# Moving casts, sums and weight preparation in a hybrid encoder layer: seven edits to a hand-ordered kernel

## The chip, the cores and the metric

The kernel runs on one NeuronCore of a Trainium2 chip. The metric is the device time of one execution in microseconds (us). Engines are named as in the profile: PE multiplies matrices, ACT (ScalarE), DVE (VectorE) and POOL (GpSimd) work elementwise, SP issues nearly all DMAs. Each engine works through its own instructions in the program's order; they wait for each other through semaphores.

## The reference

One layer of a bidirectional hybrid encoder over 1024 tokens of width 1024, in fp32:

```python
h = rmsnorm(x, norm_mix); proj = h @ w_in
q, k, v, r, lr_f, lr_b, u, g_a, g_b = split(proj)
# branch A: gated linear attention, 4 heads, forward and backward scan over chunks, summed
o = (gla_chunked(q, k, v, decay_f) + flip(gla_chunked(flip(q), ...)))
o = headnorm(o) * gla_norm * silu(r);  y_a = o @ w_branch_gla
# branch B: centred mean over windows 2/4/8/16 minus the token, a small matmul per group of channels
y_b = einsum('blgc,gcd->blgd', multiscale_pool(u), w_pool_group) * pool_scale
x = x + (sigmoid(g_a) * y_a + sigmoid(g_b) * y_b) @ w_out
gate, up = split(rmsnorm(x, norm_ffn) @ w_ffn_in)
x = x + (silu(gate) * up) @ w_ffn_out          # hidden width 2816
out = rmsnorm(x, norm_final)
```

## The kernel before, in words

**Products.** Every fp32 operand is cut into a high part (a cast on ACT) and a low part (operand minus high part, on DVE or POOL); `products` (L268) issues three matmuls for a pair: high by high, high by low, low by high, and `mm3` adds a call of `pump`. Large products use a seven-product form of 2 by 2 block multiplication: products number 1 to 7, each on sums or differences of blocks. Each product is 12 or 24 matmuls of 128x512.

**Who sets the order.** The order of all engines is written out by hand (`manual_schedule`). The main program issues products; work beside them is issued by generators that `pump(dt)` advances as matmuls are issued: `side` (attention, pooling), `aside` (the job lists of `prepare_beside`, one step every so many units), `pending` (weight casts) and `put_off` (`soon(delay, step)`). `settle()` issues all that was put off, `finish_side()` and `finish_beside()` all that is left of the generators.

**Slots.** Big tiles come from one pool of 39 slots. A tile that is allocated takes the slot of an older one, and its first writer waits for the last reader of that older one.

**Stages and places of the change.**

- *Attention, one head after the other (35 to 385 us).* `advance` (L758) makes the state of the next chunk: `st` on DVE, then on ACT the copy for use (`sb` or `sf`, L772) and the one to carry on (`so`, L773). `transposed_keys` (L750) makes `kt`: transposes on PE into `kp`, cast on ACT, low part on DVE. After the backward states come the scores, whose cast is `p`.
- *Gate units 0 to 9 (388 to 580 us).* Each unit is 128 columns of `w_in`, loaded as two `fraw` tiles, as seven products (`Gates.run`). Products 1, 6, 5 end in the ACT copy `ga<-ps` (L1304), which empties the bank for a later product. Units 6 to 9 also apply the pooled features: `load_pooled(g)` loads the tiles `ph` and `pl` from DRAM (L1245) and `Gates.pooling` multiplies them (`yb`). `flush` sends finished rows to DRAM (`sa_out`, `yb_out`, L501).
- *READY units.* The first two units of the FFN are prepared during the gate units: `unit_jobs` (L535) loads two `fraw` tiles of `w_ffn_in`, makes sums in them on POOL (L636), and `beside` cuts them into `uph` (ACT, L630) and `upl` (DVE, L621) and stores them in DRAM (`u_out`, L617), from where the FFN stage later loads them.
- *Branch and merged products (580 to 755 us)*: `line_make` (L1122) cuts the next piece into parts; `merged_piece` (L1204) makes sums of the merged rows `mg` (L1217 to L1219); `dh` and `dl` are the parts.
- *FFN (755 to 1180 us).* `features` (L1521) transposes the normed rows `xn` into banks `tr`, copies them to `hb` on ACT (L1535), makes block sums on DVE (L1547, L1550) and cuts them into `gh` (`cast_block`, ACT, L1513) and `gl` (`low_block`).
- *FFN output (1185 to 1377 us).* Pieces of weights (`wor`) and features (`gor`) are loaded (`load_piece`) and cut (`split_piece`) into `oh` and `ol`; `collect` adds the sums to `x` (L1860); `whole` (L1819) norms and stores the first four row blocks (`n3rs`, L1587; `scaled`, L1815; store, L1835) in steps put off with `soon`; `first_half` and `second_half` do the others.

Of the kernel before, what the change touches and what calls it, by code (L numbers as in the profile page):

```python
# [51 lines left out]
def kernel(  # L52
# [614 lines left out]
    def attention(h, q, k):  # L667
# [89 lines left out]

        def advance(old, n, d, kt, dst):  # L758

            kv = bank(ps_g, "kv")  # L760
            products(kv[:, :DV], tokens((kt[:, 0, :], kt[:, 1, :]), n), value(n))
            new = s1((DV,), "st")[:, :]
            after = factor(n, d, "after")
            if old is None:
                nc.vector.tensor_scalar(new, kv[:, :DV], after, None, op0=ALU.mult)
            else:
                nc.vector.scalar_tensor_tensor(
                    new, kv[:, :DV], after, old[:, :], op0=ALU.mult, op1=ALU.add
                )
            following = n + 1 if d == 0 else n - 1  # L770
            old = s1((DV,), "so")
            nc.scalar.activation(dst, new, AF.Copy, scale=factor(following, d, "before"))  # L772
            nc.scalar.activation(old[:, :], new, AF.Copy, scale=factor(following, d, "whole"))  # L773
            return old
# [45 lines left out]
        for n in range(NT - 1, 0, -1):  # L820
            m = n - 1
            old = advance(old, n, 1, kts[n // 4, 1], sb[m // 4][:, m % 4, :])
            if n == 7:
                apply_decay(1, 0)
            yield 1.2
            if n == 2:
                kts[0, 0] = transposed_keys(0, 0)
                yield 0.5
# [5 lines left out]
        for n in range(NT):  # L834
# [8 lines left out]
            for j, (a, b) in enumerate(terms):  # L843
                if j == len(terms) - 1 and n < NT - 1:
                    sf = s1((DV,), "sf")
                    old = advance(old, n, 0, kts[half, 0], sf[:, :])
                nc.tensor.matmul(op[:, :DV], a, b, start=False, stop=j == len(terms) - 1)
# [274 lines left out]
    def line_make():  # L1122
        n = len(made)
        if n < len(line):
            while len(loads) <= n:
                line_load()
            while len(begun_sums) <= n:
                line_sums()
            made.append(line[n][2](loads[n]))
# [74 lines left out]
    def merged_piece(p, c):  # L1204
# [6 lines left out]
        def sums():  # L1211
# [3 lines left out]
            if p == 6:  # L1215
                s3s.append(slot(s="s3"))
                sub(s3s[c][:, :, :], block(0, 0), block(1, 0))  # L1217
                padd(block(1, 0), block(1, 0), block(1, 1))
                sub(block(0, 0), block(1, 0), block(0, 0))  # L1219
            elif p == 3:  # L1220
# [124 lines left out]
    for n, run in enumerate(gate_runs):  # L1345
        zs[n] = Gates(n)
        last = n == len(gate_units) - 1
        if n == 0:
            prepare_beside(map(output_jobs, range(4)), 2.8)
        if n == 7:  # L1350
            finish_side()
            finish_beside()
            prepare_beside(map(unit_jobs, range(READY)), 3.1, 1, 2)
        if last:
            finish_beside()
        for at, (of, p) in enumerate(run):
            if not gates_ahead.step() and at in (5, 7):
                line_make()
            if n >= 6 and at == 2 and not last:
                load_pooled(n - 6)  # L1360
# [160 lines left out]
    def features(half):  # L1521
# [4 lines left out]
        def block(i, j, c):  # L1526
            return blocks[i, j][c][:, :, :]

        for k in range(KT):
            ps = bank(ps_g, "tr")  # L1530
            for i in range(4):
# [4 lines left out]
                blocks[k // 4, half][k % 4 // 2][:, k % 2, :], ps[:, :], AF.Copy, scale=g_ffn[:, k : k + 1]  # L1536
            )
            i = k % 4 // 2
            if k % 2 and half == 0:
# [3 lines left out]
            elif k % 2:  # L1543

                t = block(0, 0, i)
                if k < 4:
                    sub(t, block(0, 1, i), t)  # L1547
                    cast_block(5, i, t)
                else:
                    sub(t, block(1, 1, i), t)  # L1550
                    cast_block(6, i, t)
            elif half and k in (2, 4):
# [266 lines left out]
    def whole(ts):  # L1819
# [16 lines left out]

        steps = [(at + 9 * n, step, t) for n, t in enumerate(ts) for at, step in ((1, scale), (6, finish), (14.5, store))]
        for at, step, t in sorted(steps, key=lambda e: e[0]):
# [42 lines left out]
    for at, p in enumerate(OUT_ORDER):  # L1881
# [4 lines left out]
        for i in range(CLOSE if closing else n_of):  # L1886
# [6 lines left out]
            for m in range(4):  # L1893
# [3 lines left out]
                if m == (3 if i == n_of - 1 else 1):  # L1897
                    split_piece()

                if m == 3 and len(pieces) - n_of + CLOSE > n + 1 >= len(pieces) - 2 * CLOSE:  # L1900
                    load_piece()
# [36 lines left out]
```

## Time and profile before

| what | us |
|---|---|
| median of 3 runs (1389.67 to 1391.16) | 1390.08 |
| the profiled execution's own time | 1389.48 |
| its span in the trace | 1387.7 |
| PE busy | 1365.6 (98%) |
| DVE, POOL, ACT busy | 842.6, 752.6, 644.9 |
| mean granted clock of PE, share of full | 0.999 |

All times of the trace count from the start of the span. Rows of groups give the line of the kernel, the engine, the operation, what it writes and reads by the program's names with the number of instructions, then the shortest, median and longest duration in ns and the first and last start in us within the window asked for. Rows of waits give who waits for whom, us in total, times, the longest.

### The profile page before, as it was taken

Reading aid. Unit: us, or ns where it says so; the run is one execution under the profiler, and the core shown is the slowest. Engines: PE = TensorE matmul, PEld = TensorE weight load, DVE = VectorE, ACT = ScalarE, POOL = GpSimd, SP = SyncE. Lnnn points to the kernel's source line nnn. Section 1 sums busy time; section 2 is a strip of 40 time slices with the busy share of each in tenths; the row PEclk is TensorE's granted clock in tenths of the full one; section 3 lists DMA queues with packets and bytes.
Section 4 is the critical chain, followed back from the end, with each engine's and each line's share of the span. In section 5 each row is a group of like instructions: output and inputs, shape, how many; then the busy total and the mean of one; then the engine's idle time right before and its main releaser. Section 6 shows DMA issues by size and latency. Waiting matters only on the chain. (4 is left out here: it accounts for less than half of the span.)

```text
span 1387.7 us, 18162 instructions
## 1 busy us (share of the span) xinstructions
PE 1365.6 (98%) x6485; PEld 1143.0 (82%) x6485; DVE 842.6 (61%) x1018; ACT 644.9 (46%) x1176; POOL 752.6 (54%) x556
## 2 busy tenths in 40 slices
PE   7999999999999999999999999999999999999998
PEld 6888998988888888788887788888888888888876
DVE  6364656557835875687873866555655556344384
ACT  6465766655334544554347533333333334443253
POOL 3222617132288546668655276666666667554354
PEclk9999999999999999999999999999999999999999
DMA  6112414312478677996516355555444447966452
GB/s 224 31 47 60 142 52 134 105 55 77 137 214 288 198 228 242 369 405 224 186 61 241 116 175 175 174 175 175 148 146 142 145 140 273 390 244 215 169 209 93
DMA packets 166586, 243.60 MB, mean 176 GB/s; under 512 B 10936, under 2 KB 95968, under 8 KB 166496
## 3 DMA queue, kind: packets, MB, share of 16 engines
q1 hardware_dynamic: 166352, 242.18, 51.7%
q8 instruction: 51, 0.84, 0.2%
q14 instruction: 39, 0.32, 0.1%
q10 hardware_dynamic: 144, 0.26, 0.0%
HBM read 164.55 MB, written 77.86 MB: 175 GB/s over the span
## 5 line engine op out<-in xcount | busy, mean ns | idle before, releaser
L198 POOL TENSOR_TENSOR wl<-fs,wh 128x512 fp32r<-128x512 f32 x120 | 167.0, 1395 | 152.5 <-ACT wh L197 100.2
L271 PE MATMUL ps<-gh,wh 128*128 128x512 f32 x616 | 240.4, 390 | 0.0
L271 PE MATMUL ps<-gl,wh 128*128 128x512 f32 x616 | 239.8, 389 | 0.0
L271 PE MATMUL ps<-gh,wl 128*128 128x512 f32 x616 | 239.7, 389 | 0.0
L198 POOL TENSOR_TENSOR wl<-fraw,wh 128x512 fp32r<-128x512 f32 x90 | 128.8, 1432 | 64.4 <-ACT wh L197 62.0
L271 PE MATMUL ps<-hh,wh 128*128 128x512 f32 x376 | 151.6, 403 | 0.0
L198 POOL TENSOR_TENSOR ol<-gor,oh 128x1024 fp32r<-128x1024 f32 (+1 forms) x42 | 103.1, 2461 | 84.2 <-ACT oh L197 67.5
L271 PE MATMUL ps<-hh,wl 128*128 128x512 f32 x376 | 146.9, 391 | 0.6 <-POOL wl L198 0.6
L271 PE MATMUL ps<-hl,wh 128*128 128x512 f32 x376 | 146.6, 390 | 0.0
L271 PEld LDWEIGHTS ps<-gl,wh 128*128 128x128 f32 x616 | 115.7, 188 | 24.0 <-DVE gl L1517 0.3
L271 PEld LDWEIGHTS ps<-gh,wl 128*128 128x128 f32 x616 | 115.6, 188 | 23.9
L271 PEld LDWEIGHTS ps<-gh,wh 128*128 128x128 f32 x616 | 115.7, 188 | 23.8
L271 PE MATMUL ps<-oh,oh 128*128 128x512 f32 x308 | 119.9, 389 | 0.9 <-DVE x L1860 0.9
L271 PE MATMUL ps<-oh,ol 128*128 128x512 f32 x308 | 119.8, 389 | 0.0
L271 PE MATMUL ps<-ol,oh 128*128 128x512 f32 x308 | 119.8, 389 | 0.0
L198 POOL TENSOR_TENSOR wl<-raw,wh 128x512 fp32r<-128x512 f32 x40 | 54.5, 1374 | 117.0 <-ACT wh L197 108.7
L198 POOL TENSOR_TENSOR wl<-wraw,wh 128x512 fp32r<-128x512 f32 x56 | 89.9, 1633 | 45.6 <-ACT wh L197 36.4
L198 DVE TENSOR_TENSOR ol<-wor,oh 128x1024 fp32r<-128x1024 f32 (+1 forms) x42 | 69.1, 1673 | 40.8 <-ACT oh L197 37.1
L197 ACT CAST wh<-fs 128x512 fp32r<-128x512 f32 x120 | 73.7, 615 | 29.0 <-DVE fs L935 28.0
L271 PEld LDWEIGHTS ps<-hh,wl 128*128 128x128 f32 x376 | 70.6, 188 | 16.0 <-POOL wl L198 1.1
L271 PEld LDWEIGHTS ps<-hh,wh 128*128 128x128 f32 x376 | 70.7, 188 | 13.4 <-ACT wh L197 0.4
L271 PEld LDWEIGHTS ps<-hl,wh 128*128 128x128 f32 x376 | 70.8, 188 | 13.1
(259 smaller groups left out, 3121.8 us busy)
## 6 DMA issues: line engine op xcount, KB each, us to landing
fraw<-in_w_ffn_in_dram SPq DMA_DIRECT2D x44, 512.0 KB, 6.1
gor<-g_out SPq DMA_DIRECT2D x35, 512.0 KB, 4.6
g_out<-s SPq DMA_DIRECT2D x44, 256.0 KB, 2.3
raw<-in_w_in_dram SPq DMA_DIRECT2D x40, 256.0 KB, 5.0
fraw<-in_w_in_dram SPq DMA_DIRECT2D x20, 512.0 KB, 6.6
wor<-t_out SPq DMA_DIRECT2D x20, 512.0 KB, 6.7
g_out<-g SPq DMA_DIRECT2D x33, 256.0 KB, 2.4
x<-in_x_dram SPq DMA_DIRECT2D x16, 512.0 KB, 4.4
```

What stands on the lines that cost most here:

```text
L197: nc.scalar.copy(hi, src)
L198: eng.tensor_tensor(lo, src, as_f32(hi), op=ALU.subtract)
L271: nc.tensor.matmul(ps, a[i], b[j], start=first and n == 0, stop=last and n == 2, skip_group_check=onto)
```

## The change

1. `advance` gets `ends`: at the last chunk of either direction the state to carry on (`so`), which nothing reads, is not made. Eight ACT instructions fall away.
2. The keys of the first half are transposed one chunk earlier in the backward direction (after n = 3).
3. In `merged_piece` for product 6 the third sum is put off with `soon(4)`, behind a low part `dl`; `line_make` issues what was put off right after the sums that it makes itself.
4. The preparation of the READY units starts in unit 6 after four products, not at the start of unit 7.
5. In `features(1)` a block's cast `gh` is issued behind the next `hb` copy.
6. In `whole` the steps of the row blocks are 8 units apart, not 9.
7. In the FFN output one piece is loaded more at n = 9, and one loaded and cut more at n = 10, so that the pieces are cut one further ahead from there.

```diff
-        def advance(old, n, d, kt, dst):
+        def advance(old, n, d, kt, dst, ends=False):
...
             following = n + 1 if d == 0 else n - 1
+            nc.scalar.activation(dst, new, AF.Copy, scale=factor(following, d, "before"))
+            if ends:
+                return None
             old = s1((DV,), "so")
-            nc.scalar.activation(dst, new, AF.Copy, scale=factor(following, d, "before"))
             nc.scalar.activation(old[:, :], new, AF.Copy, scale=factor(following, d, "whole"))
...
-            old = advance(old, n, 1, kts[n // 4, 1], sb[m // 4][:, m % 4, :])
+            old = advance(old, n, 1, kts[n // 4, 1], sb[m // 4][:, m % 4, :], m == 0)
...
-            if n == 2:
+            if n == 3:
                 kts[0, 0] = transposed_keys(0, 0)
...
-                    old = advance(old, n, 0, kts[half, 0], sf[:, :])
+                    old = advance(old, n, 0, kts[half, 0], sf[:, :], n == NT - 2)
...
-            while len(begun_sums) <= n:
-                line_sums()
+            if len(begun_sums) <= n:
+                while len(begun_sums) <= n:
+                    line_sums()
+                settle()
...
-                sub(block(0, 0), block(1, 0), block(0, 0))
+                soon(4, partial(sub, block(0, 0), block(1, 0), block(0, 0)))
...
-        if n == 7:
-            finish_side()
-            finish_beside()
-            prepare_beside(map(unit_jobs, range(READY)), 3.1, 1, 2)
         if last:
             finish_beside()
         for at, (of, p) in enumerate(run):
             if not gates_ahead.step() and at in (5, 7):
                 line_make()
+            if n == 6 and at == 4:
+                finish_side()
+                finish_beside()
+                prepare_beside(map(unit_jobs, range(READY)), 3.1, 1, 2)
             if n >= 6 and at == 2 and not last:
                 load_pooled(n - 6)
...
+        waiting = []
         for k in range(KT):
...
+            if waiting:
+                waiting.pop()()
...
-                    cast_block(5, i, t)
+                    waiting.append(partial(cast_block, 5, i, t))
...
-                    cast_block(6, i, t)
+                    waiting.append(partial(cast_block, 6, i, t))
+                    if k == KT - 1:
+                        waiting.pop()()
...
-        steps = [(at + 9 * n, step, t) for n, t in enumerate(ts) for at, step in ((1, scale), (6, finish), (14.5, store))]
+        steps = [(at + 8 * n, step, t) for n, t in enumerate(ts) for at, step in ((1, scale), (6, finish), (14.5, store))]
...
+                if m == 3 and n in (9, 10):
+                    load_piece()
+                    if n == 10:
+                        split_piece()
```

How this moves instructions is seen in the order of the engines. First SP in gate unit 6, before: `pl` is the second tile of the pooled features of group 0, the rows of L535 are the two loads of the first READY unit, those of L927 the raw weights of gate unit 8; a row ends with the engines and DMA queues that it waits for.

```order
L1245 DMA pl_975_4984<-p_out_3941 128x1024 [waits DVE_49,Pool_49]
L501 DMA sa_out_3939<-ga_925_4773 256x1x512
L501 DMA sa_out_3939<-ga_932_4800 256x1x512 [waits DMAHW7_49,Activation_49]
L1249 DMA wpr_987_5068<-in_w_pool_group_dram 128x256
L1259 DMA p_out_3941<-ph_944_4862 128x1024 [waits DMAHW1_49,Activation_49]
L1259 DMA p_out_3941<-pl_945_4863 128x1024 [waits DMAHW2_49,DVE_49]
L535 DMA fraw_997_5121<-in_w_ffn_in_dram 128x8x128 [waits DMAHW3_49,Pool_49]
L535 DMA fraw_998_5122<-in_w_ffn_in_dram 128x8x128 [waits DMAHW6_49,DMAHW4_49]
L927 DMA fraw_1000_5130<-in_w_in_dram 128x8x128 [waits DMAHW5_49,DMAHW1_49]
L927 DMA fraw_1001_5132<-in_w_in_dram 128x8x128 [waits DMAHW2_49]
L1245 DMA ph_1009_5159<-p_out_3941 128x1024 [waits DMAHW7_49,DVE_49,Pool_49]
L1245 DMA pl_1010_5160<-p_out_3941 128x1024 [waits DMAHW0_49,PE_49]
```

And SP at the same place with the change:

```order
L535 DMA fraw_976_5028<-in_w_ffn_in_dram 128x8x128 [waits Pool_49]
L535 DMA fraw_977_5029<-in_w_ffn_in_dram 128x8x128 [waits DMAHW7_49,DMAHW5_49,PE_49]
L501 DMA sa_out_3923<-ga_917_4757 256x1x512
L501 DMA sa_out_3923<-ga_924_4784 256x1x512 [waits DMAHW1_49,Activation_49]
L1253 DMA wpr_981_5056<-in_w_pool_group_dram 128x256 [waits DMAHW2_49]
L1263 DMA p_out_3925<-ph_936_4846 128x1024 [waits DMAHW3_49,Activation_49]
L1263 DMA p_out_3925<-pl_937_4847 128x1024 [waits DMAHW4_49,DVE_49]
L929 DMA fraw_994_5117<-in_w_in_dram 128x8x128 [waits DMAHW0_49]
L929 DMA fraw_995_5119<-in_w_in_dram 128x8x128 [waits DMAHW6_49,DVE_49,Pool_49]
L1249 DMA ph_1005_5151<-p_out_3925 128x1024 [waits DMAHW7_49,DMAHW3_49]
L1249 DMA pl_1006_5152<-p_out_3925 128x1024 [waits DMAHW4_49]
L617 DMA u_out0_4_515<-uph_991_5109 128x512 [waits DMAHW1_49,Activation_49]
```

The two READY loads have moved ahead of the stores of the gate rows and of the pooled features; the second one now has a wait for PE, namely for the last product that reads the `pl` tile of group 0, whose slot it takes. The `pl` load of the next group had such a wait before and has none now. The first store of a READY part now directly follows.

Second, ACT in gate unit 7 with the change (`ps` and `ga` are the bank and the row of products 1, 6 and 5, `wh` the casts of the gate weights, `wph` that of the pool weights). Before, the four `uph` rows were not here, and the other eight stood in the same order.

```order
L197 CAST wh_987_5090<-fraw_954_4932 128x512 [waits PE_49,Pool_49]
L630 CAST uph_991_5109<-fraw_977_5029 128x512 [waits DMAHW7_49,DMAHW4_49]
L1308 COPY ga_993_5115<-ps_990_5096 128x512 [waits DMAHW3_49,DMAHW4_49,DMAHW0_49,PE_49]
L197 CAST wh_996_5121<-fs_989_5094 128x512 [waits DVE_49,Pool_49]
L630 CAST uph_999_5136<-fraw_976_5028 128x512 [waits DMAHW6_49,DMAHW3_49]
L1308 COPY ga_1001_5143<-ps_998_5125 128x512 [waits DMAHW1_49]
L197 CAST wh_1002_5145<-fraw_955_4934 128x512 [waits DMAHW3_49,Pool_49]
L630 CAST uph_1007_5164<-fraw_976_5028 128x512
L1316 ACTIVATE ga_962_4959<-ps_951_4913 128x512
L630 CAST uph_1010_5182<-fraw_977_5029 128x512 [waits DMAHW2_49,Pool_49]
L197 CAST wph_1012_5186<-wpr_981_5056 128x256
L197 CAST wh_1014_5190<-fs_1004_5149 128x512 [waits DVE_49,Activation_49]
```

The first cast of a READY part reads the second load and stands ahead of the first `ga` copy of unit 7; the fourth one waits for a DMA, the store of an earlier part that frees its buffer. Behind these rows come a fifth `uph` and the second `ga` copy of the bank `ps_990`.

Third, ACT in the second half's features, before (`hb` copies of transposed rows, `gh` casts of blocks, `g` the silu of the first FFN products):

```order
L1535 ACTIVATE hb_1466_7246<-tr_1471_7259,cols_173 128x512 [waits PE_49]
L1513 CAST gh_1472_7266<-hb_1405_6983 128x1024 [waits DVE_49]
L1535 ACTIVATE hb_1467_7247<-tr_1474_7272,cols_173 128x512 [waits PE_49]
L1673 ACT_TABLE_LOAD
L1673 ACTIVATE g_1447_7167<-g_1447_7167 128x512 [waits DVE_49]
L1535 ACTIVATE hb_1467_7247<-tr_1478_7292,cols_173 128x512 [waits PE_49]
L1513 CAST gh_1479_7299<-hb_1406_6984 128x1024 [waits DVE_49]
L1535 ACTIVATE hb_1468_7248<-tr_1481_7305,cols_173 128x512 [waits PE_49]
L1535 ACTIVATE hb_1468_7248<-tr_1482_7315,cols_173 128x512 [waits PE_49]
L1513 CAST gh_1483_7322<-hb_1405_6983 128x1024 [waits DVE_49]
L1673 ACTIVATE g_1449_7169<-g_1449_7169 128x512 [waits DVE_49]
L1535 ACTIVATE hb_1469_7249<-tr_1488_7338,cols_173 128x512 [waits PE_49]
```

and with the change:

```order
L1540 ACTIVATE hb_1458_7230<-tr_1463_7243,cols_173 128x512 [waits PE_49]
L1540 ACTIVATE hb_1459_7231<-tr_1464_7253,cols_173 128x512 [waits PE_49]
L1517 CAST gh_1465_7259<-hb_1397_6967 128x1024 [waits DVE_49]
L1682 ACT_TABLE_LOAD
L1682 ACTIVATE g_1439_7151<-g_1439_7151 128x512 [waits DVE_49]
L1540 ACTIVATE hb_1459_7231<-tr_1470_7276,cols_173 128x512 [waits PE_49]
L1540 ACTIVATE hb_1460_7232<-tr_1471_7286,cols_173 128x512 [waits PE_49]
L1517 CAST gh_1472_7292<-hb_1398_6968 128x1024 [waits DVE_49]
L1540 ACTIVATE hb_1460_7232<-tr_1474_7299,cols_173 128x512 [waits PE_49]
L1682 ACTIVATE g_1441_7153<-g_1441_7153 128x512 [waits DVE_49]
L1540 ACTIVATE hb_1461_7233<-tr_1478_7319,cols_173 128x512 [waits PE_49]
L1517 CAST gh_1479_7325<-hb_1397_6967 128x1024
```

Each cast has moved one `hb` copy back; the silu of the second `g` stands ahead of the third cast (product 6) now, and behind it before.

## The prediction

> **What bounds the kernel now.** I read the page first: busy time of each engine, then, over the whole span, the table of PE's waits, then narrow windows around each wait.
>
> ```profile
> PE 1365.6 (98%) x6485; PEld 1143.0 (82%) x6485; DVE 842.6 (61%) x1018; ACT 644.9 (46%) x1176; POOL 752.6 (54%) x556
> ```
> ```profile
> PE vps L428 <- DMA rows<-in_b_decay_bwd_dram: 7.0, 1, 7.0
> PE tr L1532 <- ACT hb L1535: 2.1, 2, 1.6
> PE op L271 <- ACT p L197: 1.2, 2, 0.6
> PE ps L271 <- ACT ga L1304: 1.1, 2, 0.7
> PE ps L271 <- DVE x L1860: 0.9, 1, 0.9
> PE op L271 <- DVE p L198: 0.9, 4, 0.2
> PE ps L271 <- DVE dl L162: 0.7, 1, 0.7
> ```
>
> The matrix engine is busy 98% of the span. The change removes no matmul, so it can win only time in which PE waits, and it can lose without limit. In the second fence each row is: who waits, for whom, us in total, times, longest. The 7.0 us at the start is untouched. The other rows hold 6.9 us; counted from matmul start to matmul start against the usual 0.23 us, as I count below, they cost about 1.4 (`ga`), 0.9 (`dl`), 2.4 (`hb`), 1.1 (`x`) and 3.4 in the heads. The 0.2% that a measurement can tell from no change is 2.8 us.
>
> **The READY units, half a gate unit sooner.** Their purpose in the profile is the `ga` row: in unit 9 the remaining `uph` casts are drained in one go, the ACT copy `ga` stands behind them, and PE waits twice. Issued sooner, the casts are spread and I book the 1.4 us as gained. But the order of SP shows a new wait: the second weight load of the pair now waits for PE. Its slot is the one of `pl` of pool group 0, and the last reader is the product `yb` inside gate unit 7. The trace of before has that product, and has a load that was waiting for just this release:
>
> ```profile
> L535 SPq DMA_DIRECT2D fraw<-in_w_ffn_in_dram x2: 928/1165/1402, 510.4 to 511.4; - x2
> L271 PE MATMUL yb<-pl,wph x1: 393/393/393, 524.5 to 524.5; 128*128 128x512 f32 x1
> L1245 SPq DMA_DIRECT2D pl<-p_out x1: 339/339/339, 524.9 to 524.9; - x1
> DMA to landing us min/median/max: 4.8/4.8/4.8
> L630 ACT CAST uph<-fraw x7: 610/622/622, 528.9 to 542.5; 128x512 fp32r<-128x512 f32 x7
> L1304 ACT COPY ga<-ps x3: 588/588/589, 519.1 to 527.9; 128x512 f32<-128x512 f32 x3
> L271 PE MATMUL ps<-trh,wh x1: 389/389/389, 525.0 to 525.0; 128*128 128x512 f32 x1
> ```
>
> In before the two loads went out at 510.4 and 511.4, and `pl` of the next group left at 524.9, as soon as the product of 524.5 was through, and landed 4.8 us later. In the changed order the second raw load has that place: issued at 524.9, landed at 529.7. On ACT, which works in order, the first `uph` cast reads just this load and now stands **ahead** of the `ga` copy that ran at 519.1. So that copy comes at 529.7 + 0.62 + 0.59 = 530.9. The product that starts at 525.0 adds onto the bank that this copy empties. **First wait: 530.9 - 525.0 = 5.9 us.** Nothing ahead of 525.0 on PE needs anything behind the blocked cast, so PE stands there once, and not earlier.
>
> What is queued behind the load: on SP two `sa_out` stores, pool weights, two `p_out` stores, two raw loads of gate unit 8, `ph` and `pl` of group 1 and only then the `u_out` stores of the READY parts. Before issued the same ten sizes (nine of 512 KB, one of 128 KB) from 505.0 on:
>
> ```profile
> DMA packets 5218, 4.83 MB, mean 293 GB/s; under 512 B 158, under 2 KB 4321, under 8 KB 5217
> p_out<-pl SPq DMA_DIRECT2D x1, 512.0 KB, 5.0
> ```
> ```profile
> L1245 SPq DMA_DIRECT2D pl<-p_out x1: 339/339/339, 505.0 to 505.0; - x1
> ```
> ```profile
> L927 SPq DMA_DIRECT2D fraw<-in_w_in_dram x2: 1564/2088/2612, 513.6 to 516.3; - x2
> ```
> ```profile
> L197 ACT CAST wph<-wpr x1: 397/397/397, 525.0 to 525.0; 128x256 fp32r<-128x256 f32 x1
> ```
> ```profile
> u_out<-upl SPq DMA_DIRECT2D x14, 256.0 KB, 3.1
> ```
> ```profile
> L271 PE MATMUL ps<-trh,wh x1: 389/389/389, 533.1 to 533.1; 128*128 128x512 f32 x1
> ```
>
> The first of these fences is the window 505.0 to 521.5: 4.83 MB at 293 GB/s are 16.5 us. The fourth `uph` cast takes the buffer of the first `upl`, so it waits until that part's `u_out` store has landed, and that store lies behind the ten. I take the landing as 17 us after 524.9 (ten transfers of 16.5 us and 0.5 MB more, less what the releases leave closer together). Behind this cast on ACT stand `wph` (0.40), a `wh` cast (0.62), a fifth `uph` (0.62) and then the next `ga` copy (0.59): 541.9 + 0.62 + 0.40 + 0.62 + 0.62 + 0.59 = 544.8. PE needs it for the matmul that started at 533.1. **Both waits together: 544.8 - 533.1 = 11.7 us**, 5.8 more than the first alone. Bounds for the landing: below, the stores leave as soon as SP got through the ten in before (last issue begun at 516.3 and 1.6 long, so 12.8 us after 505.0) and land after 3.1, 15.9 us; above, the ten at 293 GB/s and then 0.5 MB at the same rate and a small tail, 19 us. So 10.6 to 13.7. Later casts wait for stores too, but by the same sums the next `ga` copies (unit 8) come 5 us ahead of need, and the one of product (8,6) about at need.
>
> [...]
>
> **Heads.** Eight `so` of 0.49 us fall away, two of each head, one of them just ahead of the cast of `p`; against it a key cast and its low part move ahead of one more state step.
>
> ```profile
> L773 ACT ACTIVATE so<-st,fac x56: 492/493/507, 100.2 to 321.0; 128x256 f32<-128x256 f32 x56
> L197 ACT CAST kt<-kp x3: 567/575/592, 91.7 to 107.9; 128x512 fp32r<-128x512 f32 x3
> ```
>
> Where the next state waits for ACT (heads 1 and 3, with the 0.6 us `p` waits) the cast of `p` comes 0.6 and 0.7 sooner (the `so` and the rest of a key cast); in heads 0 and 2 a copy or key cast (0.57) newly precedes it and costs 0.25 and 0.3. Sum **-0.8**, between -2.0 and +0.6.
>
> **The third sum behind a low part.**
>
> ```profile
> L1217 DVE TENSOR_TENSOR s<-mg,mg x1: 1864/1864/1864, 679.3 to 679.3; 128x1024 f32<-128x1024 f32 x1
> L1219 DVE TENSOR_TENSOR mg<-mg,mg x1: 1226/1226/1226, 683.7 to 683.7; 128x1024 f32<-128x1024 f32 x1
> L162 DVE TENSOR_TENSOR dl<-mg,dh x2: 1217/1222/1226, 684.8 to 686.0; 128x1024 fp32r<-128x1024 f32 x2
> ```
>
> The low part `dl` ended at 686.0 because it stood behind a sum that itself waited for POOL until 683.7. Ahead of that sum it ends near 682.4, and the wait goes: **-0.9**. The sum's own reader, the second half of the same product, has 5 us left.
>
> **Features of the second half.** PE's transposes wait for `hb` copies that free their banks; the copies stand behind a `gh` cast that waits for a DVE sum.
>
> ```profile
> L1535 ACT ACTIVATE hb<-tr,cols x8: 669/681/709, 756.3 to 770.0; 128x512 f32<-128x512 f32 x8
> L1513 ACT CAST gh<-hb x6: 1040/1046/1050, 758.9 to 774.4; 128x1024 fp32r<-128x1024 f32 x6
> L1550 DVE TENSOR_TENSOR hb<-hb,hb x2: 1225/1226/1226, 766.6 to 770.7; 128x1024 f32<-128x1024 f32 x2
> ```
> ```profile
> L1672 DVE TENSOR_TENSOR g<-ps,g x3: 681/683/686, 758.8 to 771.8; 128x512 f32<-128x512 f32 x3
> L1673 ACT ACTIVATE g<-g x3: 626/628/632, 761.8 to 772.9; 128x512 f32<-128x512 f32 x3
> ```
> ```profile
> L1517 DVE TENSOR_TENSOR gl<-hb,gh x1: 1226/1226/1226, 773.0 to 773.0; 128x1024 fp32r<-128x1024 f32 x1
> L271 PE MATMUL ps<-gl,wh x1: 496/496/496, 774.3 to 774.3; 128*128 128x512 f32 x1
> ```
>
> With the cast behind the copy the fourth copy ends at 762.5 and the fifth at 763.1 instead of 766.0: the waits of 2.4 go. But what ends the stage is the other way round. The last rows show that the low part of product 6 (773.0 to 774.2) was ready just when its matmul started, 774.3. In the new order the silu of `g` stands ahead of both product-6 casts and waits for the DVE row `g`, which now stands behind a low part and a sum; hand over hand the casts end at 770.1 and 773.6 (before 769.0 and 773.0) and the last low part at 774.8. PE arrives 2.4 sooner and waits until 774.9. **+0.5** rather than -2.4, between -1.5 and +1.
>
> **Closing: steps of 8 instead of 9, pieces one further ahead.**
>
> ```profile
> L1815 DVE SCALAR_TENSOR_TENSOR x<-x,n3rs,gfin x2: 2878/2882/2885, 1343.0 to 1345.8; 128x512 f32<-128x512 f32 x2
> L1860 DVE TENSOR_TENSOR x<-ps,x x4: 674/674/679, 1349.7 to 1351.5; 128x512 f32<-128x512 f32 x4
> ```
> ```profile
> L1815 DVE SCALAR_TENSOR_TENSOR x<-x,n3rs,gfin x4: 750/751/753, 1373.0 to 1383.2; 128x512 f32<-128x512 f32 x4
> ```
>
> The `x` wait ends a DVE chain that has no gap over half a us from 1325 on; ahead of the sums `x` it holds five full low parts, a half one and the same scaled rows before and after, only the half one sooner. **0**, between -1.1 and +0.5. [...]
>
> **Sum.** 11.7 - 1.4 - 0.8 - 0.9 + 0.5 + 0 = +9.1 on the profiled execution's 1389.48 (span 1387.7 and 1.8 around it): 1398.6. The median shown, 1390.08, lies 0.6 above that execution: 1399.2.
>
> **Rivals.** (1) **One wait only** (0.17): the store lands within 11.2 us of the release, so that the second copy is ready when PE, 5.9 late, comes (533.1 + 5.9 - 2.9 - 524.9). For it: the DMA rows are empty before 524.9, so the queue starts from nothing; against it: nine of the ten must move ahead of the store, and at 293 GB/s eleven us carry only 3.2 MB of their 4.8. +5.9 - 2.6 = +3.3: 1393.4. (2) **A third wait** (0.08): the copy of (8,6) stands behind `uph` casts that wait for stores which SP issues only after `pl` of group 2; my sums leave it under half a us. +1 to +3 more: 1400 to 1402. (3) **Faster** (0.11): the second load is not held, because its slot is free by the time SP comes to it. Place: the same `ga` copy; it decides at a landing of 523.8 (525.0 - 0.62 - 0.59); before that there is no wait and the gains stay: -1.4 - 0.8 - 0.9 + 0.5 = -2.6, 1387.5, and down to -6.6, 1383.5, if the features' and the closing waits also go. Against it: the release is a matmul of 524.5. (4) **The change does not do what it says** (0.03): casts spread, waits replaced one for one, within 0.2%.
>
> **Numbers.** Forecast 1399.2 with 0.61, its own range 1396.5 to 1402.5. The range down to 1392.5 takes in the one-wait case and leaves out the faster one: 1392.5 to 1402.5. Faster 0.11; same 0.06 (case 4 and the low end of case 1); slower 0.83.
>
> **What would show it.** In the changed profile: an SP wait of some 19 us ended by PE `yb`; the load L535 issued at 524.9; a PE wait `ps <- ACT ga` of 5 to 6 us near 525 and one near 539 of about as much; no `ga` wait in unit 9; no `dl` wait; the `hb` waits gone and a wait for `gl` near 772 in their place. It is wrong if PE's new waits are absent, or if the time lies under 1392.

## The result and the profile after

The changed kernel takes **1404.73 us** (median of 5 runs, 1403.75 to 1406.82) against 1390.08 for the kernel before: ratio 1.0106, 95% interval 1.0091 to 1.0121. The sign is that of the forecast; the time lies 5.5 us above it and 2.2 above the end of its range. The profiled execution took 1406.82 with a span of 1405.1, which is 17.4 more than before.

Busy times and the table of PE's waits, over the whole span of the changed kernel:

```profile
PE 1372.3 (98%) x6485; PEld 1146.1 (82%) x6485; DVE 835.4 (59%) x1018; ACT 641.2 (46%) x1168; POOL 755.5 (54%) x556
```
```profile
PE ps L271 <- ACT ga L1308: 12.8, 3, 5.0
...
PE ps L271 <- ACT gh L1517: 0.8, 1, 0.8
PE ps L271 <- DVE gl L1521: 0.8, 1, 0.8
PE op L271 <- ACT p L197: 0.6, 2, 0.4
PE ps L271 <- ACT hb L1540: 0.4, 1, 0.4
```

(The rows left out, for `vps`, for `p` on DVE and for `x`, are within 0.3 us of those before.) The `ga` row went from 1.1 to 12.8 us, in three waits and not two; the `dl` row is gone; the `hb` waits of 2.1 became waits for `hb`, `gh` and `gl` of 2.0 together. PE's busy time is 6.7 us longer with the same 6485 matmuls. That was not in the forecast, and the windows around the waits show it. First the changed kernel, behind the first and behind the second wait; then the kernel before. Columns: stretch, its length, busy time and number of instructions of PE, PEld, DVE, ACT, POOL, the clock granted to PE as a share of full, DMA share, GB/s.

```profile
530.00:535.10 5.10, 5.10 (x13) 4.00 (x14) 2.24 (x3) 3.11 (x6) 4.56 (x4) 0.53 1.00 336
545.50:548.60 3.10, 3.10 (x8) 2.45 (x9) 3.10 (x4) 0.95 (x2) 3.10 (x3) 0.52 0.82 247
```
```profile
530.00:535.10 5.10, 5.10 (x24) 4.24 (x23) 3.96 (x6) 2.19 (x5) 2.85 (x3) 1.00 0.56 207
```

After each wait PE ran at half the clock for a while (granted clock 0.53 in 530.0 to 535.1, 0.52 in 545.5 to 548.6 and, behind the third wait, 0.53 in 572.4 to 576.0): 13 matmuls in the 5.1 us behind the first wait, where the kernel before fits 24. PE's rows there (start, length, operation) begin so, the first with the wait before it:

```profile
530.00 0.79 PE L271 MATMUL ps<-trh,wh 128*128 128x512 f32 x1 [4.99 <-ACT ga L1308]
530.59 0.63 PE L271 MATMUL ps<-trl,wh 128*128 128x512 f32 x1
531.01 0.63 PE L271 MATMUL ps<-trh,wl 128*128 128x512 f32 x1
```

Start to start they are 0.43 us apart instead of 0.23. I count as slow a matmul with more than 0.36 us to the start of the next one: 11 behind the first wait (2.3 us too much), 6 behind the second (1.4), 7 behind the third (1.6).

The waits themselves are those of the prediction. SP's waits in 500 to 530, the two loads of L535, and ACT's rows (start, length) ahead of the first, the second and the third wait:

```profile
SPq L535 <- PE yb L271: 16.4, 1, 16.4
SPq L535 <- DMA pl<-p_out: 2.9, 1, 2.9
```
```profile
L535 SPq DMA_DIRECT2D fraw<-in_w_ffn_in_dram x2: 383/406/428, 505.3 to 524.8; - x2
```
```profile
528.84 0.62 ACT L630 CAST uph<-fraw 128x512 fp32r<-128x512 f32 x1 [12.90 <-DMA fraw<-in_w_ffn_in_dram]
529.36 0.58 ACT L1308 COPY ga<-ps 128x512 f32<-128x512 f32 x1
...
542.97 0.62 ACT L630 CAST uph<-fraw 128x512 fp32r<-128x512 f32 x1 [9.42 <-DMA u_out<-upl]
543.49 0.40 ACT L197 CAST wph<-wpr 128x256 fp32r<-128x256 f32 x1
543.80 0.61 ACT L197 CAST wh<-fs 128x512 fp32r<-128x512 f32 x1
544.32 0.61 ACT L630 CAST uph<-fraw 128x512 fp32r<-128x512 f32 x1
544.84 0.57 ACT L1308 COPY ga<-ps 128x512 f32<-128x512 f32 x1
...
569.40 0.62 ACT L630 CAST uph<-fraw 128x512 fp32r<-128x512 f32 x1 [6.55 <-DMA u_out<-upl]
...
571.75 0.58 ACT L1308 COPY ga<-ps 128x512 f32<-128x512 f32 x1
```

The second load goes out at 524.8, 19.3 us after SP came to it, and its cast starts 4.0 us later; the fourth `uph` cast waits for a store until 543.0, and the `ga` copy ends at 545.4. At 569.4 the same happens once more.

To see which stage pays, I take the first PE rows of the stages: the gate stage starts with the first `ps<-trh`, the branch stage with the first `ps<-dh` (before, then after).

```profile
386.15 0.39 PE L271 MATMUL ps<-trh,wh 128*128 128x512 f32 x1
```
```profile
586.84 0.39 PE L271 MATMUL ps<-dh,wh 128*128 128x512 f32 x1
```
```profile
386.03 0.39 PE L271 MATMUL ps<-trh,wh 128*128 128x512 f32 x1
```
```profile
604.24 0.39 PE L271 MATMUL ps<-dh,wh 128*128 128x512 f32 x1
```

Read in the same way from first start to first start (`ps<-gh` for the FFN, `ps<-oh` for the output), in us:

| stage | before | after |
|---|---|---|
| heads (first product to gate stage) | 379.2 | 379.3 |
| gate stage | 200.7 | 218.2 |
| branch and merged products | 157.4 | 156.9 |
| FFN | 425.7 | 426.2 |
| FFN output (to the last matmul) | 210.4 | 210.3 |

The whole loss is in the gate stage, +17.5.

### The profile page after: what moved, and what is told of

It reads as the page before. It is cut to its first block, busy times and chain, and to the rows that moved or that the text cites. A ratio compares the mean times of both kernels' runs of the same rounds, so it can differ in the third digit from the quotient of the medians.

```text
span 1405.1 us, 18150 instructions
## 1 busy us (share of the span) xinstructions
PE 1372.3 (98%) x6485; PEld 1146.1 (82%) x6485; DVE 835.4 (59%) x1018; ACT 641.2 (46%) x1168; POOL 755.5 (54%) x556
## 5 line engine op out<-in xcount | busy, mean ns | idle before, releaser
L198 POOL TENSOR_TENSOR ol<-gor,oh 128x1024 fp32r<-128x1024 f32 (+1 forms) x42 | 100.2, 2391 | 83.7 <-ACT oh L197 61.9
L198 POOL TENSOR_TENSOR wl<-wraw,wh 128x512 fp32r<-128x512 f32 x56 | 93.5, 1698 | 44.6 <-ACT wh L197 44.5
L198 DVE TENSOR_TENSOR ol<-wor,oh 128x1024 fp32r<-128x1024 f32 (+1 forms) x42 | 62.3, 1495 | 66.9 <-ACT oh L197 51.8
```

Source lines behind the costliest of these rows:

```text
L198: eng.tensor_tensor(lo, src, as_f32(hi), op=ALU.subtract)
```

## The experiments

Unless an edit says otherwise it is made in the changed kernel. "Gate stage" is the time above, from each kernel's own trace.

**READY alone, and all but READY.**

```diff
 only_ready:    the kernel before, with edit 4 alone
 all_but_ready: the changed kernel, without edit 4
```

> The kernel before with edit 4 alone (READY units from unit 6). Theory: this edit alone makes the loss. The changed kernel's trace has three PE waits for `ga` (5.2, 4.9 and 3.3 us), after each of them 8 to 12 matmuls at 0.43 instead of 0.23 us (2.5, 1.7 and 1.7 us), and no wait in unit 9 (-1.4): +17.9 by these sums, so 1406 to 1408, about 1 us above the changed kernel, because the gains in the heads (-0.4) and at `dl` (-0.9) are missing. Rival: the other edits share the loss (the sums of the trace leave about 1 us unexplained); then it is below the changed kernel, 1403 or less.

> The changed kernel with the READY units started where they were before, at unit 7; the other six edits in. Theory: -0.4 in the heads, -0.9 at `dl`, +0.2 in the features, 0 in the closing: 1 us below the kernel before, ratio 0.9992, waits for `ga` in unit 9 still there (1.1 us). Rival: the other edits lose too, 1 us or more above the kernel before.

Measured: 1405.59, ratio 1.0109 (1.0095 to 1.0122), gate stage 217.2; and 1390.55, ratio 0.9998 (0.9990 to 1.0007), gate stage 201.7. Edit 4 makes the whole loss. The other six together cannot be told from no change, nor from the 1 us expected of them: the expected ratio, 0.9992, lies in the interval.

**The slot, not the time.** Two kernels in which the second load gets another slot:

```diff
 swap:
-            (None, 4, a22), (None, 1, a11), (None, 2, a12), (partial(padd, a22, a21, a22), 5, a22),
+            (None, 1, a11), (None, 2, a12), (None, 4, a22), (partial(padd, a22, a21, a22), 5, a22),
 start_65, in the kernel before, edit 4 with another place:
+            if n == 6 and at == 5:
```

> The changed kernel with the first three jobs of a READY unit in the order a11, a12, a22 instead of a22, a11, a12: the first two casts read the first load, which is there in time, and the cast that reads the held load stands behind the first `ga` copy of unit 7. So the first wait (5.2 us, and 2.5 us of slow matmuls) goes. Theory (the end of the second wait hangs on SP's queue, which starts at 524.9, not on PE): PE comes 7.7 us sooner to product 7 of unit 7 and waits there 12 us instead of 4.9; the time stays within 1 us of the changed kernel, 1404 to 1405.5. Rival (each wait is a cost by itself): 7.7 us less, 1397.

> The kernel before with the READY units started in unit 6 one product later than in the change (after five products, behind the two `sa_out` stores on SP); the other edits not in. By the order on SP the second load then waits for a store only and takes another slot, not that of `pl`. Theory (the earlier start costs only through the slot that the load gets): no wait for `ga` near 525, the load goes out before 516; the fourth cast can still wait for a store that stands behind a `pl` load which waits for `yb` at 524.9, so a wait of up to 3 us near 533 is possible; without it the time is 1389 to 1391, with it up to 1395. Rival (to cast the READY parts this early is too much for ACT, whichever slot): waits as in the change, 1400 to 1406.

(In swap the low part of a22 is taken when the sum has already overwritten it, so one part of each READY unit is not the reference's.) The two loads of L535 and PE's `ga` row, swap first:

```profile
L535 SPq DMA_DIRECT2D fraw<-in_w_ffn_in_dram x2: 383/405/427, 504.4 to 517.7; - x2
```
```profile
PE ps L271 <- ACT ga L1308: 8.5, 2, 5.6
```
```profile
L535 SPq DMA_DIRECT2D fraw<-in_w_ffn_in_dram x2: 389/500/610, 507.4 to 510.6; - x2
```
```profile
PE ps L271 <- ACT ga L1304: 2.9, 1, 2.9
```

Swap took 1400.50, ratio 1.0065 (1.0051 to 1.0079): neither number expected, because the edit did more than I meant. The second load fell on a slot that a DVE sum frees, and went out 132.6 us after the start of the gate stage instead of 138.8 (517.7 - 385.1 and 524.8 - 386.0), 6.2 sooner. The first wait went, and the second ended at 152.9 instead of 159.4 by the same count, 6.5 sooner. So its end moves with the held load, as the theory says, and not with PE, which came to it at 147.3 instead of 154.7. In start_65 the load is released by a store and goes out at 510.6: no wait near 525 or 533, 1392.01, ratio 1.0010 (1.0001 to 1.0019), gate stage 203.8; what is left is one wait of 2.9 us at 557.4 behind a later `uph` cast, and 9 slow matmuls. A start one product later costs 1 to 2 us where the change's costs 15.

**Stores past the held load.**

```diff
-                nc.sync.dma_start(*pair)
+                (nc.gpsimd if put == 1 else nc.sync).dma_start(*pair)
```

> The changed kernel with the stores of the READY parts (`u_out`) issued by POOL's queue, so that they no longer stand behind the held load on SP. Nothing else is changed; the second load is still released by the product `yb` at 524. Theory: the first wait stays (5 us and up to 2.5 us of slow matmuls), since the cast still reads that load; the second and the third wait go, because the fourth and the later casts wait only for stores that are issued at once: about 11.5 us less than the changed kernel (4.9 + 1.7 + 3.3 + 1.7), 1393. Rival: the casts crowd ACT wherever they stand, or POOL, which now issues 28 stores beside its low parts, holds PE at `wl` instead: 1400 or more.

Measured: 1420.35, ratio 1.0209 (1.0190 to 1.0228). The stores did not go out at once, so the expected gain did not come. POOL's first stores and the low part that follows them, and the cast on ACT that waits for them:

```profile
533.69 0.75 POOL L617 DMA_DIRECT2D u_out<-uph  x1
534.45 0.55 POOL L617 DMA_DIRECT2D u_out<-upl  x1
...
542.86 1.67 POOL L198 TENSOR_TENSOR wl<-fs,wh 128x512 fp32r<-128x512 f32 x1 [4.18 <-ACT wh L197]
```
```profile
541.34 0.62 ACT L630 CAST uph<-fraw 128x512 fp32r<-128x512 f32 x1 [8.89 <-DMA u_out<-upl]
```

Counted from the start of the gate stage (384.8 here), the first store leaves only 1.2 us sooner than on SP, because POOL comes to it behind its own low parts and sums, and the cast that waits starts only 0.35 sooner, 6.9 us after the `upl` store left: the DMA engines are full there (share 1.07 in 534.0 to 541.4). The later ones stand behind a low part that waits for `wh`, which stands on ACT behind the cast that waits for the stores. This fits a second wait that hangs on the transfers that pile up behind the held load, as the prediction's 16.5 us had it. How much of it SP's order alone makes stays open, since no run issued the stores at once.

**The third wait.**

```diff
-            if n >= 6 and at == 2 and not last:
+            if n >= 6 and at == (4 if n == 8 else 2) and not last:
                 load_pooled(n - 6)
```

> The changed kernel with the tiles `ph` and `pl` of pool group 2 loaded two products later in unit 8, so that on SP they stand behind the first three pairs of `u_out` stores of the second READY unit instead of ahead of them. Theory (the third wait comes from these stores, which stand on SP behind a `pl` load that waits for `yb` at 560.9): the third wait (3.1 us) and the slow matmuls behind it (2.2 us) go or shrink to under 1 us, the first two stay: 3 to 5 us less than the changed kernel, 1400 to 1402. Rival (the transfers are simply too many at this place, the order does not matter): third wait 2 us or more, 1404 to 1405.

```profile
PE ps L271 <- ACT ga L1308: 9.5, 2, 5.2
```

Two waits are left. 1403.41, ratio 1.0092 (1.0078 to 1.0106), gate stage 214.4, 3.8 less than the changed kernel's. The stage has what was expected; the time, 1.3 us less, lies above the expected 1400 to 1402, and its interval overlaps with that of the changed kernel. The third wait does come from stores behind the `pl` load that waits for `yb`.

**Idle PE and the slow matmuls.** First waits made where no READY work is, in the kernel before:

```diff
-                nc.scalar.copy(self.row(part[0])[:, part[1], :], ps)
+                for _ in range(1 + (HOLDS.get(self.n, 0) if p == 1 else 0)):
+                    nc.scalar.copy(self.row(part[0])[:, part[1], :], ps)
 pause_up:   HOLDS = {1: 13, 2: 15, 3: 16, 4: 17, 5: 18, 6: 20}
 pause_down: HOLDS = {1: 22, 2: 18, 3: 17, 4: 16, 5: 15, 6: 14}
```

> The kernel before, with the ACT copy `ga` of product 1 written 13, 15, 16, 17, 18 and 20 times more in gate units 1 to 6 (the same copy again, the result is the same): product 6 of the unit then waits for the last of them. No READY work is near. Copies follow each other in 0.48 us and there are 4.6 us of slack: waits of 1.6, 2.6, 3.1, 3.6, 4.0 and 5.0 us. Theory (idle PE makes the matmuls after it slow): 7 to 13 matmuls at 0.43 us after each wait over 3 us, none after the 1.6; in between it can go either way, since 2.4 us had none and 2.9 us had eight so far. The time is 1390 plus 20 of waits plus 6 to 10 of slow matmuls, 1416 to 1420. Rival (they come from READY's traffic): no matmul at 0.43 us, 1410.

> The same with 22, 18, 17, 16, 15 and 14 more copies in units 1 to 6, so that length and place are not mixed up: waits of 6.0, 4.0, 3.6, 3.1, 2.6 and 2.1 us. Theory: 7 to 13 slow matmuls after each wait over 3 us wherever it stands, fewer or none after 2.1 and 2.6; the number does not grow with the wait. Rival: the number grows with the length of the wait, or depends on the unit.

One run each: 1437.81 and 1438.65. The waits came out longer than planned (I had the slack too large):

| pause_up: wait, us | 3.3 | 4.6 | 5.1 | 5.8 | 6.4 | 7.6 |
|---|---|---|---|---|---|---|
| slow matmuls (us too much) | 8 (1.6) | 7 (1.5) | 10 (2.2) | 10 (2.2) | 9 (2.0) | 13 (2.8) |
| **pause_down: wait, us** | 8.8 | 6.4 | 5.7 | 5.2 | 4.6 | 3.9 |
| slow matmuls (us too much) | 8 (1.7) | 7 (1.6) | 9 (2.0) | 11 (2.4) | 14 (2.9) | 7 (1.4) |

Every wait has them, 7 to 14, with no READY traffic near and no more of them after a longer wait. At the shortest wait the clock fell after the work had begun again, between the matmul of 412.42 and that of 413.35 (pause_up):

```profile
412.08 0.50 PE L271 MATMUL ps<-trh,wh 128*128 128x512 f32 x1 [3.28 <-ACT ga L1308]
412.42 0.39 PE L271 MATMUL ps<-trl,wh 128*128 128x512 f32 x1
...
413.35 0.63 PE L271 MATMUL ps<-trh,wl 128*128 128x512 f32 x1
```
```profile
412.10:417.00 4.90, 4.90 (x15) 3.87 (x16) 0.00 (x0) 2.88 (x6) 4.38 (x4) 0.65 0.14 54
```

Then the other way round, the idle time filled:

```diff
 fill, fill_in:
+            if (n, of, p) == (7, 6, 4):
+                for _ in range(20):
+                    nc.tensor.matmul(zs[6].yb[:, :], wpool[0][1][:, :P], pools[0][0][:, 0, :], start=True, stop=True)
 fill: 26 and 10 more onto the bank of product 3 of units 7 and 8, after the product
 fill_in: the same 26 and 10 inside the product; fill_last: 11 inside that of unit 8 alone
+            for _ in range(EXTRA.pop() if k == 3 and EXTRA else 0):
+                nc.tensor.matmul(ps[:, :], unit(p, 0)[0], right[p][0][0][:, 0, :], start=False, stop=False, skip_group_check=True)
```

> The changed kernel with idle time of PE filled: 20 matmuls of 128x512 ahead of product 6 of unit 7, 26 ahead of product 7 of unit 7, 10 ahead of product 7 of unit 8, where PE waits for `ga`; they overwrite sums, so the rows of pool group 0 and some of the gates are not the reference's. Theory: the slow matmuls follow from the idle time (they come after 5.0, 4.7 and 3.1 us without a matmul, and nowhere after the 1.7 us and less in the trace of before), and the end of the second wait hangs on SP's queue: with no idle time over 1 us no matmul runs at 0.43 us; the 2.5 us after the first wait are given back as a longer second wait, the 1.7 after the second and the 1.7 after the third are won: 3.4 us below the changed kernel, 1401.3. Rival 1 (all three are won): 5.9 below, 1398.8. Rival 2 (the slow matmuls come from the transfers and casts of the READY units around them, not from the idle time): matmuls at 0.43 us at the same places and no gain.

> The changed kernel with 20 more matmuls ahead of product 6 of unit 7, and 26 and 10 more inside product 3 of units 7 and 8 (added onto its own sum, so that no other reader has to be awaited, which held the earlier filled kernel up); the rows that they feed are not the reference's. They stand where PE would be idle. Theory (idle PE slows the matmuls behind it, and the end of the second wait hangs on the transfers behind the held load): no matmul at 0.43 us near 530, 545 and 572; the 2.3 us after the first wait only make the second wait longer, the 1.4 after the second and the 2.2 after the third are won: 3.6 us less than the changed kernel, 1401. Rival: all 5.9 us are won, 1399; or none.

> The changed kernel with 11 more matmuls inside product 3 of unit 8, onto its own sum (that row is not the reference's), where PE would wait the third time; nothing else. Theory: the third wait still ends near 572.4, no matmul at 0.43 us behind it, and since no later wait can take the 2.2 us up, the time is 2 us below the changed kernel, 1402.5. Rival (what is won there is lost in a later wait): 1404 to 1405.

Fill, 1428.69 (ratio 1.0272, 1.0258 to 1.0286), was flawed: its added matmuls had to wait for the DVE reader of the bank, 12.7 and 8.9 us. Its first filling held: no slow matmul at 530. Fill_in has the fillings without that; its windows:

```profile
524.80:530.30 5.50, 4.82 (x22) 3.57 (x20) 0.83 (x2) 1.27 (x3) 0.00 (x0) 1.00 0.77 259
530.30:535.20 4.90, 4.90 (x21) 4.04 (x22) 1.83 (x2) 3.10 (x6) 4.37 (x4) 1.00 1.03 363
...
546.10:549.00 2.90, 2.88 (x12) 2.10 (x12) 2.90 (x4) 1.01 (x2) 2.90 (x3) 1.00 0.80 243
```

The full clock throughout, among the same transfers, and no slow matmul: idleness is the cause. Yet product 7 of unit 7 starts at 546.1 (545.5 in the changed kernel), and the kernel takes 1406.12, ratio 1.0119 (1.0105 to 1.0132). What was won behind the first wait only made the second longer, as expected; what was won behind the second went into a new wait of 1.2 us for DVE, which I put down to the longer product 3. Fill_last has no slow matmul behind the third wait (the expectations of fill_in and fill_last put 2.2 us there; by the count used here it is 1.6), and its gate stage is 215.7, 2.6 less than the changed kernel's. Of these, 1.2 are there already when the third wait ends, 186.4 and 185.2 us after the start of the stage, so 1.4 are left for the slow matmuls. Its time, 1405.82 (ratio 1.0110, 1.0096 to 1.0124), does not show that. So the trace gives the slow matmuls behind the last wait as a cost of their own, and the times leave it open.

How much idle time it took can be read from the granted clock. In the changed kernel's trace it changed at 527.98, 534.81, 545.05, 548.46, 572.36 and 575.77, which lie 6.83, 10.24, 3.41, 23.89 and 3.41 us apart, two, three, one, seven and one times 3.413. Here are three traces cut into stretches of that length (columns as above), first the changed kernel around its first wait, then pool_store around a wait of 1.9 us, then only_ready around its wait of 2.4 us:

```profile
524.57:527.98 3.41, 0.44 (x2) 0.00 (x0) 0.00 (x0) 0.00 (x0) 0.00 (x0) 1.00 0.56 167
527.98:531.39 3.41, 1.40 (x3) 1.16 (x4) 1.67 (x3) 2.14 (x4) 0.85 (x1) 0.50 1.07 406
531.39:534.81 3.42, 3.42 (x9) 2.63 (x8) 1.08 (x1) 2.13 (x4) 3.42 (x4) 0.50 0.98 311
534.81:538.22 3.41, 3.41 (x16) 2.78 (x15) 0.00 (x0) 0.00 (x0) 2.58 (x3) 1.00 1.12 329
```
```profile
556.22:559.63 3.41, 1.48 (x7) 0.91 (x6) 1.73 (x3) 0.41 (x1) 0.97 (x2) 1.00 0.93 371
559.63:563.05 3.42, 3.42 (x10) 2.68 (x9) 3.42 (x6) 2.78 (x6) 2.32 (x2) 0.50 0.86 216
```
```profile
567.88:571.30 3.42, 2.39 (x11) 1.65 (x9) 0.83 (x2) 1.58 (x4) 0.75 (x1) 1.00 0.92 352
571.30:574.71 3.41, 2.00 (x8) 1.40 (x9) 3.41 (x5) 2.39 (x5) 2.98 (x2) 1.00 0.71 264
574.71:578.12 3.41, 3.41 (x16) 2.76 (x15) 3.33 (x5) 1.66 (x3) 2.71 (x3) 1.00 1.02 392
```

The stretches at full clock with PE busy for 0.13 (0.44 of 3.41 us, changed kernel) and 0.43 of the time (1.48 of 3.41, pool_store) were followed by one at half clock; behind the stretch of the changed kernel in which PE was busy throughout (3.42 of 3.42), the full clock came back. So in these traces the length of a wait alone did not decide: the 1.9 us of pool_store fell into one such stretch, and the 2.4 us of only_ready into two, with PE busy for 0.70 and 0.59 of them, and there the clock stayed full. That the idle time within one stretch is what counts is my estimate from these rows.

**The small edits, and a better kernel.**

```diff
 no_ready_no_feat: the kernel before, with edits 1, 2, 3, 6 and 7
 every_28: as that, and
-            prepare_beside(map(unit_jobs, range(READY)), 3.1, 1, 2)
+            prepare_beside(map(unit_jobs, range(READY)), 2.8, 1, 2)
 feat_half: as every_28, with edit 5 for the casts of product 5 alone
 feat_full: as every_28, with the whole of edit 5
```

> The kernel before with the edits in the heads, at `dl` and in the closing alone (no READY units sooner, no casts behind the next copy). Theory: -0.4 in the heads, -0.9 at `dl`: 1389, and no slow matmuls behind the feature waits, which three of the five profiles with the edit of the features had and none of the five without it. Rival: these edits bring nothing that can be measured, 1390.2.

> As no_ready_no_feat, and the jobs of the READY units one every 2.8 units of pump instead of 3.1, from the same start in unit 7. Theory: the casts of the READY units are through before unit 9 without being drained at once, so the two waits for `ga` there (1.4 to 2.4 us) go, and no slot changes its release: 1387. Rival: closer casts wait for their stores and hold a `ga` copy in unit 7 or 8, 3 us and more and slow matmuls after it: 1391 or more.

> As every_28, and in the features only the casts of product 5 behind the next copy; those of product 6 at once, as before. Theory: the two `hb` waits (2.4 us) go, and since the casts of product 6 do not stand behind the silu of `g`, PE waits less for them than the 2.0 us in the changed kernel: 1 to 2 us below every_28. Rival: PE, there sooner, waits for `gh` and `gl` as long as in the changed kernel: same as every_28.

> As feat_half, but with the change's own edit of the features (the casts of product 6 behind the next copy too): the changed kernel with READY started at unit 7 as before and spaced 2.8. Theory: against feat_half the three waits for `hb`, `gh` and `gl` cost 0.8 us more and now and then 1.5 us of slow matmuls behind them: 1 to 2 us above feat_half (ratio 0.998). Rival: no difference, ratio 0.997.

| kernel | median, us | ratio to before (95%) | gate stage | FFN stage |
|---|---|---|---|---|
| no_ready_no_feat | 1389.80 | 0.9997 (0.9988 to 1.0006) | 201.9 | 426.1 |
| every_28 | 1387.02 | 0.9976 (0.9966 to 0.9985) | 199.0 | 425.7 |
| feat_half | 1385.77 | 0.9971 (0.9961 to 0.9982) | 199.0 | 425.0 |
| feat_full | 1387.87 | 0.9979 (0.9970 to 0.9988) | 200.3 | 426.2 |

Edits 1, 2, 3, 6 and 7 bring nothing that these times can tell from zero. Every_28 does what edit 4 was meant to do: from the old start, with its casts a little closer, the READY units are through before unit 9, and PE waits for no `ga` at all; 0.24% faster than before. Feat_half is the fastest run here; its gain over every_28 is inside the intervals, but the trace has it in its place (0.7 us in the FFN stage). Feat_full against feat_half is +1.1 in that stage, as expected; another 1.3 are in the gate stage, where it waits for `ga` twice (0.6 us together).

## Why the sign was right and the size wrong

| step of the prediction | forecast | measured |
|---|---|---|
| first and second wait together | +11.7 | +12.3 (545.46 - 533.1) |
| third wait, rival (2) | left out (+1 to +3) | +3.3 (3.1 of it wait) |
| matmuls at half clock behind the second and third wait | not in the sum | +3.0 (1.4 + 1.6) |
| unit-9 waits gone | -1.4 | -1.4 |
| heads | -0.8 | +0.1 (stage, one pair of traces; see below) |
| `dl` | -0.9 | -0.5 (stage) |
| features | +0.5 | +0.5 (stage) |
| closing | 0 | -0.1 (stage) |

- **The READY mechanism was right, in every link**: the SP wait (19.3 us against "some 19"), the release by `yb`, the issue at 524.8, the cast that takes the `ga` copy with it, the fourth cast behind the stores. The load landed 4.0 us after issue and not 4.8, so the first wait is 5.0 and not 5.9; the store was there 18.2 us after the release instead of 17, inside the bounds. The five ACT rows behind it took 2.4 us and not 2.85, since each starts before the one ahead of it has ended; so the two misses partly cancel, and that the sum of both waits came within 0.6 us is luck to that extent. Only_ready, swap and start_65 show that the released slot is the cause.
- **The step that failed** is the end of that part: "by the same sums the next `ga` copies (unit 8) come 5 us ahead of need, and the one of product (8,6) about at need". The copy of (8,6) came 3.1 us late. Rival (2) had named place and cause, stores behind the `pl` load of group 2, and pl_late confirmed them; its price was a little too low (at most +3, without the slow matmuls behind it), and its chance of 0.08 too small for a case whose margin the sum itself put at half a us.
- **The term that was missing**: the kernel paid for a wait of PE twice. The forecast counted a wait as the time for which PE stands; behind each wait of 3.1 us and more in the changed kernel and the two pause kernels its slow matmuls took 1.4 to 2.9 us too much. Behind the first wait it cost nothing, since the second wait, whose end is set by the transfers, took it up; this is why the two-wait sum came out right without it. Behind the second and third it was 3.0 us in the trace. The waits of before could not have shown it (1.6 us at most between products, granted clock 0.999), but its first products, behind the 7.0 us of the start, do: the rows below, of the kernel before, start 0.43 us apart, and from 13.24 on three matmuls take 0.69, 0.23 each.

```profile
11.64 0.63 PE L271 MATMUL ps<-wv,hl 128*128 128x512 f32 x1
12.07 1.05 PE L271 MATMUL ps<-wv,hh 128*128 128x512 f32 x2
13.24 0.63 PE L271 MATMUL ps<-wv,hh 128*128 128x512 f32 x2
13.93 0.39 PE L271 MATMUL ps<-wv,hh 128*128 128x512 f32 x1
```

- **Small terms**: the features came out by the forecast's mechanism, a wait for `gh` and `gl` of product 6 in place of the `hb` waits. It costs more at times: in three of nine profiles with the whole of edit 5 (all_but_ready, swap, fill) the two waits of 0.8 us, 1.3 apart, were followed by 7 to 9 slow matmuls (all_but_ready: 0.43 us from start to start from 775.77 to 778.34). The heads' gain is open: the `p` waits are shorter, 1.2 to 0.6 in the tables, the stage in this pair of traces is not. But the stage varies more than that from trace to trace, 377.0 to 379.9 in the twelve traces with these edits (mean 378.7) and 378.8 to 380.1 in the five without (mean 379.3), so a gain of some 0.6 is likely and not shown. At `dl` the 0.5 is shown: the stage takes 156.9 in all twelve traces with the edit and 157.4 to 157.5 in all five without.

The span grew by 17.4 us, 8.3 more than the forecast's sum of +9.1: 6.3 are the third wait and the slow matmuls (3.3 and 3.0), 0.6 the first two waits, 1.2 the heads, `dl` and the closing together, and 0.2 is left over. The profiled execution of the changed kernel is the longest of its five, 2.1 above their median; between the medians the forecast is 5.5 short.

## What to carry to other kernels

The load that was moved ahead in SP's queue started when its buffer was free (524.8, 19.3 us after SP had come to it), not where it stood; before moving one, look up in the trace who reads last from the slot that it gets, and what waits behind it on its queue and behind its first reader. Here a wait of PE of 3.1 us or more cost 1.4 to 2.9 us on top, unless another wait took them up, and two of 0.8 us, 1.3 apart, were followed by 7 to 9 slow matmuls in three of nine profiles; so a sum of waits needs that term, and a margin of half a us is no margin. To get work out of the way in time, closer steps from the old start did what an earlier start could not.

## What the runs showed of the hardware

- Behind waits of 3.1 to 8.8 us (changed kernel, pause_up, pause_down) PE ran at half clock: 0.43 instead of 0.23 us per 128x512 matmul, granted clock about 0.5, for 6 to 14 matmuls (3 to 6 us), and no more of them behind 8.8 us (8) than behind 3.3 (8). In pause_up the fall came 1.3 us after work had begun again.
- The length of the idle time alone set no sharp bound. 2.4 us without a matmul (only_ready) and 1.6 (kernel before, the `hb` wait that ended at 766.0) had no slow matmuls; 1.9 us had 8 once (pool_store), and two waits of 0.8 us close together had 7 to 9 in three of nine profiles.
- In the changed kernel the changes of the granted clock lay 6.83, 10.24, 3.41, 23.89 and 3.41 us apart. It fell behind a stretch of 3.41 us with PE busy for 0.13 of it (changed kernel) and behind one with 0.43 (pool_store, around the 1.9 us), and stayed full behind two with 0.70 and 0.59 (only_ready, around the 2.4 us).
- The cast that waited for a 256 KB store started 6.9 us after POOL had issued it (pool_store, DMA share 1.07 in 534.0 to 541.4) and 6.4 after SP had (542.97 - 536.6, changed kernel, share 1.04 in that time): the store did not land sooner by way of the other queue.
